# Sums of w_down's quarters formed during the first MLP product, and u kept by granule

## The chip, the cores and the metric

The kernel runs on one core of a Trainium2 chip, as one program. The metric is device time in microseconds (us), median of the runs shown; less is better. The engines are TensorE (PE, with its weight loads as PEld), VectorE (DVE), ScalarE (ACT), GpSimd (POOL) and SyncE (SP, which here only issues DMAs from a queue that it works through in order).

## The reference, cut to what matters

One inference step of a two-layer streaming encoder, for a prompt of 1024 tokens and a sample of 64 (1088 together, model width 1024). Each layer has a mixer, then cross-attention into 256 memory tokens, then a squared-ReLU MLP of width 4096. The change concerns the MLP alone:

```python
def sq_relu_mlp(h, w_up, w_down):
    return jnp.square(jax.nn.relu(h @ w_up)) @ w_down
...
x = x + cross_attn(rmsnorm(x, p['norm_cross'][layer]), mem_k[layer], mem_v[layer],
                   p['w_mq'][layer], p['w_mo'][layer])
x = x + sq_relu_mlp(rmsnorm(x, p['norm_mlp'][layer]), p['w_up'][layer], p['w_down'][layer])
```

Everything is float32. w_up is 1024x4096, w_down 4096x1024.

## The kernel before

**Precision and weights.** A float32 operand is split into a high part (an fp32r copy by ACT) and a low part (a DVE subtraction); a product is three matmuls. All weights come through one object `W` in the order of a list `plan`: `load` issues a 512 KB DMA on SP into a staging tile `st` (pool `wst`, 4 buffers), `do_split` makes the high and low parts from it (L212 on ACT, L213 on DVE) in a tile `wp` (3 buffers) or, for w_down's granules 3 to 7 of a product, `wd` (5 buffers, in the down stage's own pool). `ahead` keeps about two split tiles in front of PE.

**Order.** The code is written in program order; a tile scheduler turns it into one queue of instructions per engine, each of which runs in order, with semaphore waits between them. A tile with n buffers makes its next user wait until the release of the n-th last.

**Up stage** (`mlp_up`). Sixteen passes q, each with two w_up tiles (f = 0, 1) and three units of PE work per tile: 512 tokens of sequence half 0 and twice 288 of half 1. DVE turns a PSUM bank into `t` (L967, relu and the norm's row factor rb), ACT squares `t` into `u` (L970, L972). `u` has eight slots (four quarters, U11 to U22, and four differences T1 to T4) and two buffers. At the end of a pass POOL makes the four differences (L983, 128x544 each) and SP stores slots 0 to 6 to DRAM (L985, 1904 KB).

**The norm's rows.** PE's first unit of pass 0 is followed by `rows()`: rc is made from column sums (DVE L341, then the power -1/2 on POOL at L342), PE transposes it (L352), ACT copies it into rb. DVE's L967 of half 1 needs rb.

**Down stage** (`mlp_down`). u @ w_down is done with seven products of quarter matrices (list `SEVEN`), in two halves each, 14 steps. Step (m, half) uses four granules of weights (512 KB each, quarter (k half, n half) of w_down or a sum of quarters) and four granules of u. `load_u` reads one granule with two DMAs of 272 KB, because pass q's u lies in a DRAM tensor of its own, into `ur` (3 buffers); ACT (L259) and DVE (L262) split it into one of eight `hp` tiles. The first four granules are loaded ahead of step 0, the others during the step before. L1042, L1043, L1044 are the three matmuls; DVE adds finished banks to x. In products m = 2 to 5 a weight granule is a sum or difference of two matrices. `load` then stages both, POOL combines them (L205, 128x1024), and for m = 3 and 4 SP stores the result to DRAM (L207), because a later product reads it again:

```python
(((1, 0), "add", (1, 1)), "S1", T1, ((0, 1), (1, 1)), "add"),
(("S1", "subtract", (0, 0)), "S2", T2, ((0, 1), (1, 0), (1, 1)), "add"),
```

Both store and loads stand in SP's one queue. The stage before up is cross-attention; its last part is `project_back` with w_mo (8 weight tiles), and its tiles' space is reused by the up stage's pools.

Of the kernel before, what the change touches and what calls it, by code (L numbers as in the profile page):

```python
# [7 lines left out]
F32 = mybir.dt.float32  # L8
# [5 lines left out]
D = 1024  # L14
# [15 lines left out]
NST = 4  # L30

# [3 lines left out]
U11, U21, U22, T1, T2, T3, T4, U12 = range(8)  # L35
SEVEN = [
    (((0, 0), None, None), None, U11, ((0, 0), (0, 1), (1, 0), (1, 1)), "add"),
    (((1, 1), None, None), None, T4, ((1, 0),), "subtract"),
    (((0, 0), "subtract", (1, 0)), None, T3, ((1, 0), (1, 1)), "add"),
    (((1, 0), "add", (1, 1)), "S1", T1, ((0, 1), (1, 1)), "add"),  # L40
    (("S1", "subtract", (0, 0)), "S2", T2, ((0, 1), (1, 0), (1, 1)), "add"),
    (((0, 1), "subtract", "S2"), None, U22, ((0, 1),), "add"),
    (((0, 1), None, None), None, U21, ((0, 0),), "add"),
# [4 lines left out]
def body(ctx, tc, I, O):  # L48
# [12 lines left out]
    wst = ctx.enter_context(tc.tile_pool(name="wst", bufs=NST))  # L61
# [58 lines left out]
    def plan_mlp(l):  # L120
        for n in range(NFF):
            plan.append(((("up", l), n), "n", cols(I["w_up"][l], n * 128, 128)))
        sums = {}

        def quarter(q, g):

            w = I["w_down"][l]
            return dram(w, (4 * g + q[1]) * 128 * D + q[0] * 512, [[D, 128], [256 * D, 2], [1, 512]])

        for m, ((a, op, b), keep, *_) in enumerate(SEVEN):  # L130
            for g in range(8):
                def src(q):
                    return sums[q, g] if isinstance(q, str) else quarter(q, g)

                kept = None
                if keep:
                    kept = sums[keep, g] = scr.tile([128, 2, 512], F32, name=f"{keep}{l}_{g}")
                plan.append((("down", l, m, g), "s", (src(a), op, src(b) if op else None, kept)))

# [16 lines left out]
    class Weights:  # L156
# [5 lines left out]
        def load(self):  # L162
# [1347 lines left out]
```

## Time and profile before

| | us |
|---|---|
| median of 3 runs | 2848.53 |
| lowest, highest | 2841.72, 2851.61 |
| the profiled execution | 2846.64 |
| its span, first to last instruction | 2844.9 |
| PE busy, share of the span | 2725.1, 96% |
| DVE, ACT, POOL busy | 50%, 39%, 19% |
| mean granted TensorE clock | 0.979 |

The profiled execution is 1.9 us under the median, its span 1.7 us under its own time. Time is in the row of a group as busy us and mean ns of one instruction, then the idle time of the engine ahead of it with what ended it. A window's row gives the busy us of each engine and, behind them, the granted clock as a share of full speed. Idle time is of interest where PE waits.

### The profile page before, as it was taken

The page shows a single profiled execution, that of the slowest core. Times are in us where ns is not written, and L with a number is a line of the kernel's source. Part 1 is how long each engine was busy: PE and PEld are TensorE (multiplying, and loading weights), DVE is VectorE, ACT ScalarE, POOL GpSimd, SP SyncE. Part 2 cuts the span into 40 slices and gives each one's busy share as a digit, 9 for nine tenths or more (in the row PEclk, how much of TensorE's full clock was granted, in tenths as well). Part 3 has the DMA queues.
Part 4 walks back from the last instruction along what each step waited for, and adds up shares of the span by engine and source line. Part 5 has one row for each costly group of instructions (what it writes and reads, how often), then busy time and mean ns, then how long its engine had stood idle before and what let it go on. Part 6 is the DMA issues. An engine that isn't in the chain of part 4 may idle for free. (4 is left out here: it accounts for less than half of the span.)

```text
span 2844.9 us, 44625 instructions
## 1 busy us (share of the span) xinstructions
PE 2725.1 (96%) x18280; PEld 2545.7 (89%) x18280; DVE 1413.5 (50%) x2328; ACT 1096.5 (39%) x1929; POOL 538.4 (19%) x422
## 2 busy tenths in 40 slices
PE   8999999999999979979999999999999999799798
PEld 8978998999999979979988899889989999799798
DVE  5596756563222225445557467566522222364454
ACT  6584545343222223323337347344422222332234
POOL 3200000001222220333003013000022222123320
PEclk9999999999999989989999999999999999899899
DMA  8722232322333346777621321323223333667871
GB/s 283 221 74 82 67 105 78 105 63 87 128 128 128 130 145 222 249 262 270 185 68 28 91 64 46 93 89 93 60 100 127 128 127 127 213 223 253 281 259 71
DMA packets 355921, 395.13 MB, mean 139 GB/s; under 512 B 47632, under 2 KB 268832, under 8 KB 351620
## 3 DMA queue, kind: packets, MB, share of 16 engines
q1 hardware_dynamic: 346820, 365.23, 39.1%
q0 software_dynamic: 8896, 27.06, 2.9%
q8 instruction: 143, 2.34, 0.3%
q14 instruction: 62, 0.51, 0.1%
HBM read 299.74 MB, written 92.61 MB: 138 GB/s over the span
## 5 line engine op out<-in xcount | busy, mean ns | idle before, releaser
L242 PE MATMUL mm<-hpH,wp 128*128 128x288 f32 (+2 forms) x5952 | 1420.4, 328 | 3.9 <-DVE U L569 2.3
L242 PEld LDWEIGHTS mm<-hpH,wp 128*128 128x128 f32 x5952 | 1013.4, 188 | 83.2 <-DVE U L569 2.7
L242 PE MATMUL mm<-hpL,wp 128*128 128x288 f32 (+2 forms) x2976 | 926.2, 327 | 3.2 <-DVE hpL L317 3.2
L242 PEld LDWEIGHTS mm<-hpL,wp 128*128 128x128 f32 x2976 | 561.1, 189 | 42.4 <-DVE hpL L317 4.0
L212 ACT ACTIVATE wp<-st 128x1024 fp32r<-128x1024 f32 x282 | 297.6, 1058 | 615.4 <-PE mm L242 456.3
L213 DVE TENSOR_TENSOR wp<-st,wp 128x1024 fp32r<-128x1024 f32 x282 | 347.6, 1234 | 195.9 <-ACT wp L212 195.6
L967 DVE SCALAR_TENSOR_TENSOR t<-mm,rb 128x288 f32<-128x288 f32 (+1 forms) x184 | 99.2, 539 | 515.3 <-PE mm L242 515.3
L983 POOL TENSOR_TENSOR u<-u 128x544 f32<-128x544 f32 x128 | 218.2, 1715 | 537.2 <-ACT u L972 534.7
L205 POOL TENSOR_TENSOR st<-st 128x1024 f32<-128x1024 f32 x64 | 164.2, 2566 | 430.4 <-DMA st<-in_w_down_dram 262.0
L262 DVE TENSOR_TENSOR uhl<-ur,uhl 128x1088 fp32r<-128x1088 f32 x112 | 155.0, 1387 | 167.7 <-ACT uhl L259 167.5
L259 ACT ACTIVATE uhl<-ur 128x1088 fp32r<-128x1088 f32 x112 | 123.6, 1106 | 225.3 <-DMA ur<-u 223.2
L1042 PE MATMUL s<-uhl,wd 128*128 128x256 f32 x560 | 160.8, 288 | 31.0 <-ACT uhl L259 31.0
L1043 PE MATMUL s<-uhl,wd 128*128 128x256 f32 x560 | 161.7, 289 | 8.0 <-DVE uhl L262 8.0
L1044 PE MATMUL s<-uhl,wd 128*128 128x256 f32 x560 | 159.9, 286 | 0.0
L970 ACT ACTIVATE u<-t 128x512 f32<-128x512 f32 x64 | 40.4, 632 | 301.4 <-DVE t L967 301.4
L242 PE MATMUL s<-hpH,wp 128*128 128x288 f32 (+1 forms) x576 | 141.4, 330 | 0.0
L1042 PEld LDWEIGHTS s<-uhl,wd 128*128 128x128 f32 x560 | 109.2, 195 | 32.7 <-ACT uhl L259 32.7
L212 ACT ACTIVATE wd<-st 128x1024 fp32r<-128x1024 f32 x70 | 72.8, 1051 | 156.9 <-POOL st L205 62.5
L1042 PE MATMUL s<-uhl,wp 128*128 128x256 f32 x336 | 96.5, 291 | 36.8 <-ACT uhl L259 36.8
L213 DVE TENSOR_TENSOR wd<-st,wd 128x1024 fp32r<-128x1024 f32 x70 | 92.1, 1325 | 59.0 <-ACT wd L212 33.2
L1043 PEld LDWEIGHTS s<-uhl,wd 128*128 128x128 f32 x560 | 109.5, 196 | 9.7 <-DVE uhl L262 9.7
L342 POOL TENSOR_TENSOR rc<-rc,mhalf 128x4 f32<-128x4 f32 (+1 forms) x21 | 23.4, 1122 | 490.6 <-DVE rc L341 490.6
(364 smaller groups left out, 4725.8 us busy)
## 6 DMA issues: line engine op xcount, KB each, us to landing
st<-in_w_down_dram SPq DMA_DIRECT2D x144, 512.0 KB, 4.5
u<-u SPq DMA_DIRECT2D x32, 1904.0 KB, 5.9
ur<-u SPq DMA_DIRECT2D x224, 272.0 KB, 4.9
st<-in_w_up_dram SPq DMA_DIRECT2D x64, 512.0 KB, 4.1
st<-in_w_mq_dram SPq DMA_DIRECT2D x32, 512.0 KB, 3.6
st<-in_w_mo_dram SPq DMA_DIRECT2D x32, 512.0 KB, 3.6
S<-st SPq DMA_DIRECT2D x32, 512.0 KB, 5.9
st<-S SPq DMA_DIRECT2D x32, 512.0 KB, 4.3
```

The costliest lines, as they stand in the source:

```text
L205: pool.tensor_tensor(st, st, sts[1], getattr(OP, op))
L212: act.activation(wt[:, 0], st, AF.Copy)
L213: dve.tensor_tensor(wt[:, 1], st, f32(wt[:, 0]), OP.subtract)
L242: pe.matmul(ps, a, b, start=i == 0, stop=i == len(terms) - 1)
L259: act.activation(h, src, AF.Copy)
L262: dve.tensor_tensor(l, src, f32(h), OP.subtract)
L967: dve.scalar_tensor_tensor(t[:, :bn], ps[:, :bn], 0.0, nm.rb[:, b0:b0 + bn], OP.max, OP.mult)
L970: act.activation(slots[:, :, :256], t.rearrange("p (a b) -> p a b", a=2), AF.Square)
L983: pool.tensor_tensor(u[:, to], u[:, a], u[:, b], OP.subtract)
L1042: pe.matmul(ps, wl, uh, start=first, stop=False)
L1043: pe.matmul(ps, wh, ul, start=False, stop=False)
L1044: pe.matmul(ps, wh, uh, start=False, stop=half == 1 and g == 3 and k == 1)
```

## The change

The seven products stay, and PE's work is the same. `weights_sums(q)`, called in each up pass, loads 256 rows of w_down (two DMAs of 512 KB) into one tile `quarters` (1 buffer), POOL makes four 128x512 sums and differences in place (L947 to L950: S1, S3, S2, S4), and SP stores the tile (1 MB) to a DRAM tensor `sums`. In the down stage every weight granule is then one staged tile: 56 loads in a layer instead of 88 (72 from w_down, 16 of stored sums), with no POOL instruction (before, 32 in a layer) and no store of a sum (before, 16). u lies in DRAM by granule, so `load_u` is one DMA of 544 KB; the stores of u and of the sums go through a list `todo`, which `store()` empties at a later place in the code. The four first granules of u are loaded and split within the last up pass, after its second unit, which is why `ur` now lives in a pool around both stages. `wst` has 3 buffers instead of 4, in all stages.

```diff
+S2, S3, S4, S1 = range(4)
 SEVEN = [
-    (((0, 0), None, None), None, U11, ((0, 0), (0, 1), (1, 0), (1, 1)), "add"),
-    (((1, 1), None, None), None, T4, ((1, 0),), "subtract"),
-    (((0, 0), "subtract", (1, 0)), None, T3, ((1, 0), (1, 1)), "add"),
-    (((1, 0), "add", (1, 1)), "S1", T1, ((0, 1), (1, 1)), "add"),
-    (("S1", "subtract", (0, 0)), "S2", T2, ((0, 1), (1, 0), (1, 1)), "add"),
-    (((0, 1), "subtract", "S2"), None, U22, ((0, 1),), "add"),
-    (((0, 1), None, None), None, U21, ((0, 0),), "add"),
+    ((0, 0), U11, ((0, 0), (0, 1), (1, 0), (1, 1)), "add"),
+    ((1, 1), T4, ((1, 0),), "subtract"),
+    (S3, T3, ((1, 0), (1, 1)), "add"),
+    (S1, T1, ((0, 1), (1, 1)), "add"),
+    (S2, T2, ((0, 1), (1, 0), (1, 1)), "add"),
+    (S4, U22, ((0, 1),), "add"),
+    ((0, 1), U21, ((0, 0),), "add"),
...
-    wst = ctx.enter_context(tc.tile_pool(name="wst", bufs=NST))
+    wst = ctx.enter_context(tc.tile_pool(name="wst", bufs=3))
...
-        for m, ((a, op, b), keep, *_) in enumerate(SEVEN):
+        w = I["w_down"][l]
...
             for g in range(8):
-                def src(q):
-                    return sums[q, g] if isinstance(q, str) else quarter(q, g)
-
-                kept = None
-                if keep:
-                    kept = sums[keep, g] = scr.tile([128, 2, 512], F32, name=f"{keep}{l}_{g}")
-                plan.append((("down", l, m, g), "s", (src(a), op, src(b) if op else None, kept)))
-
+                if isinstance(q, int):
+                    src = sums[l][g][:, q]
+                else:
+                    src = dram(w, (4 * g + q[1]) * 128 * D + q[0] * 512, [[D, 128], [256 * D, 2], [1, 512]])
+                plan.append((("down", l, m, g), "s", [(slice(0, 128), None, src)]))
+    sums = [[scr.tile([128, 4, 2, 512], F32, name=f"sums{l}_{g}") for g in range(8)] for l in range(2)]
...
-            if kind == "s":
-                a, op, b, kept = pieces
-                srcs = [a] if b is None else [a, b]
-                if self.staged + len(srcs) > NST:
-                    return False
-                sts = []
-                for src in srcs:
-                    st = wst.tile([128, 1024], F32, tag="st", name="st")
-                    nc.sync.dma_start(st.rearrange("p (k n) -> p k n", n=512), src)
-                    sts.append(st)
-                self.stage[self.loaded] = sts
-                self.staged += len(srcs)
-                self.loaded += 1
-                return True
...
-            sts = self.stage.pop(self.split)
+            st = self.stage.pop(self.split)
             key, kind, pieces = plan[self.split]
-            st = sts[0]
-            if len(sts) > 1:
-                a, op, b, kept = pieces
-                pool.tensor_tensor(st, st, sts[1], getattr(OP, op))
-                if kept is not None:
-                    nc.sync.dma_start(kept, st.rearrange("p (k n) -> p k n", n=512))
...
-            self.staged -= len(sts)
+            self.staged -= 1
...
-    def mlp_up(l, norms, p):
+    def load_u(us, p, m, g):
+        ur = p.tile([128, 2, TH], F32, tag="ur", name="ur", bufs=3)
+        nc.sync.dma_start(ur, us[g][:, SEVEN[m][1]])
+        t = hpp.tile([128, 4, NT2], F32R, tag="hp", name="uhl").rearrange("p a b -> p (a b)")
+        h, lo = (t[:, 2 * TH * i:2 * TH * i + 2 * TH] for i in range(2))
+        split(h, lo, ur.rearrange("p a b -> p (a b)"))
+        return t[:, :4 * TH].rearrange("p (i k t) -> p i k t", i=2, k=2)
+
+    def mlp_up(l, norms, p, outer):
         blocks = [(0, 0, 512), (1, 0, 288), (1, 288, 288)]
-        us = []
+        us = [scr.tile([128, 7, 2, TH], F32, name=f"u{l}_{g}") for g in range(8)]
+        todo, first = [], []
+
+        def weights_sums(q):
+
+            a = p.tile([128, 4, 512], F32, tag="quarters", name="quarters", bufs=1)
+            for i in range(2):
+                nc.sync.dma_start(a[:, 2 * i:2 * i + 2],
+                                  I["w_down"][l][256 * q + 128 * i:256 * q + 128 * i + 128]
+                                  .rearrange("p (h n) -> p h n", h=2))
+
+            pool.tensor_tensor(a[:, 3], a[:, 1], a[:, 3], OP.add)
+            pool.tensor_tensor(a[:, 1], a[:, 0], a[:, 1], OP.subtract)
+            pool.tensor_tensor(a[:, 0], a[:, 3], a[:, 0], OP.subtract)
+            pool.tensor_tensor(a[:, 2], a[:, 2], a[:, 0], OP.subtract)
+            todo.append((sums[l][q // 2][:, :, q % 2], a))
+
+        def store():
+            while todo:
+                nc.sync.dma_start(*todo.pop(0))
...
                 wts[f] = W.get((("up", l), 2 * q + f))
                 for o in order[f]:
                     unit(*o)
+                    if q == 15 and o == (1, 0):
+                        store()
+                        first = [load_u(us, outer, 0, g) for g in range(4)]
                 W.ahead()
+                if f == 0:
+                    store()
             for to, a, b in ((T1, U12, U11), (T3, U22, U12), (T2, U22, T1), (T4, T2, U21)):
                 pool.tensor_tensor(u[:, to], u[:, a], u[:, b], OP.subtract)
-            d = scr.tile([128, 7, TH], F32, name=f"u{l}_{q}")
-            nc.sync.dma_start(d, u[:, :7])
-            us.append(d)
-        return us
-
-    def mlp_down(l, us, last, p):
+            todo.append((us[q // 2][:, :, q % 2], u[:, :7]))
+            weights_sums(q)
+        store()
+        return us, first
+
+    def mlp_down(l, us, first, last, p, outer):
...
-        ready = {}
-
-        def load_u(m, g):
-            ur = p.tile([128, 2, TH], F32, tag="ur", name="ur", bufs=3)
-            for i in range(2):
-                nc.sync.dma_start(ur[:, i], us[2 * g + i][:, SEVEN[m][2]])
-            t = hpp.tile([128, 4, NT2], F32R, tag="hp", name="uhl").rearrange("p a b -> p (a b)")
-            h, lo = (t[:, 2 * TH * i:2 * TH * i + 2 * TH] for i in range(2))
-            split(h, lo, ur.rearrange("p a b -> p (a b)"))
-            ready[m, g] = t[:, :4 * TH].rearrange("p (i k t) -> p i k t", i=2, k=2)
+        ready = {(0, g): t for g, t in enumerate(first)}
...
-        for g in range(4):
-            load_u(0, g)
         for i, (m, half) in enumerate(steps):
...
                     if after is not None and s == 0:
                         W.ahead(c + 1)
-                        load_u(after[0], 4 * after[1] + c)
+                        g = 4 * after[1] + c
+                        ready[after[0], g] = load_u(us, outer, after[0], g)
...
-            with phase(f"up{l}") as p:
-                us = mlp_up(l, [nexts[1], prepared(1, G_MLP + l)], p)
-            with phase(f"down{l}") as p:
+            with phase(f"mlp{l}") as outer:
+                with phase(f"up{l}") as p:
+                    up = mlp_up(l, [nexts[1], prepared(1, G_MLP + l)], p, outer)
...
-                mlp_down(l, us, last, p)
+                with phase(f"down{l}") as p:
+                    mlp_down(l, *up, last, p, outer)
```

The change also reorders queues. At the end of layer 0's cross-attention and the start of up, POOL's queue before is (o32 belongs to the last attention head, rc to the norm of half 1, u to the passes):

```order
L926 TENSOR_TENSOR o32_6191<-o32_6191 128x2x64
L342 TENSOR_TENSOR rc_6765<-rc_6765,mhalf_123 128x4
L342 TENSOR_TENSOR rc_6765<-rc_6765,mhalf_123 64x1
L983 TENSOR_TENSOR u_6780<-u_6780 128x544 x4
L983 TENSOR_TENSOR u_6965<-u_6965 128x544 x4
L983 TENSOR_TENSOR u_7150<-u_7150 128x544 x4
```

and now:

```order
L900 TENSOR_TENSOR o32_6175<-o32_6175 128x2x64
L947 TENSOR_TENSOR quarters_6958<-quarters_6958 128x512
L948 TENSOR_TENSOR quarters_6958<-quarters_6958 128x512
L949 TENSOR_TENSOR quarters_6958<-quarters_6958 128x512
L950 TENSOR_TENSOR quarters_6958<-quarters_6958 128x512
...
L950 TENSOR_TENSOR quarters_7534<-quarters_7534 128x512
L316 TENSOR_TENSOR rc_6752<-rc_6752,mhalf_107 128x4
L316 TENSOR_TENSOR rc_6752<-rc_6752,mhalf_107 64x1
L947 TENSOR_TENSOR quarters_7726<-quarters_7726 128x512
```

Between the two fences' o32 and rc there now stand the sums of passes 0 to 3, four instructions each. The u rows of the passes, one after another before, now alternate with the sums; for pass 6, tile `u_7925`:

```order
L990 TENSOR_TENSOR u_7925<-u_7925 128x544
L947 TENSOR_TENSOR quarters_9646<-quarters_9646 128x512
L948 TENSOR_TENSOR quarters_9646<-quarters_9646 128x512
L949 TENSOR_TENSOR quarters_9646<-quarters_9646 128x512
L950 TENSOR_TENSOR quarters_9646<-quarters_9646 128x512
L990 TENSOR_TENSOR u_7925<-u_7925 128x544 x3
L990 TENSOR_TENSOR u_8117<-u_8117 128x544
L947 TENSOR_TENSOR quarters_9858<-quarters_9858 128x512
```

One of pass 6's differences stands ahead of the fifteenth set of sums and three behind it.

SP's queue at the same place, the last w_mo tiles and the first w_up tiles, before:

```order
L194 DMA st_6311<-in_w_mo_dram 128x8x128
L194 DMA st_6368<-in_w_mo_dram 128x8x128
L194 DMA st_6425<-in_w_mo_dram 128x8x128
L194 DMA st_6482<-in_w_up_dram 128x8x128
L194 DMA st_6539<-in_w_up_dram 128x8x128
```

and now:

```order
L174 DMA st_6295<-in_w_mo_dram 128x8x128
L943 DMA quarters_6958<-in_w_down_dram 128x1024 x2
L174 DMA st_6352<-in_w_mo_dram 128x8x128
L955 DMA sums0_0_84<-quarters_6958 512x1x512
L174 DMA st_6409<-in_w_mo_dram 128x8x128
L943 DMA quarters_7150<-in_w_down_dram 128x1024 x2
L174 DMA st_6466<-in_w_up_dram 128x8x128
L955 DMA sums0_0_84<-quarters_7150 512x1x512
L174 DMA st_6523<-in_w_up_dram 128x8x128
L943 DMA quarters_7342<-in_w_down_dram 128x1024 x2
L174 DMA st_6580<-in_w_up_dram 128x8x128
```

Loads of `quarters` and stores of `sums` stand between the weight loads, each load of `quarters` behind the store of the one before.

SP's queue at the change from up to down, before (the u stores of passes 14 and 15, then the loads of the first granules `ur`):

```order
L985 DMA u0_14_9555<-u_9372 128x3808
L175 DMA st_9734<-in_w_down_dram 128x2x512
L175 DMA st_9773<-in_w_down_dram 128x2x512
L985 DMA u0_15_9740<-u_9557 128x3808
L999 DMA ur_9746<-u0_0_6963 128x544
L999 DMA ur_9746<-u0_1_7148 128x544
L999 DMA ur_9752<-u0_2_7333 128x544
L999 DMA ur_9752<-u0_3_7518 128x544
```

and now (the stores of passes 14 and 15 write `u0_7`, and `ur_9732` is granule 3):

```order
L955 DMA u0_7_6774<-u_9461 896x1x544
L928 DMA ur_9732<-u0_3_6770 128x1088
L928 DMA ur_9911<-u0_4_6771 128x1088
L928 DMA ur_9946<-u0_5_6772 128x1088
L928 DMA ur_9981<-u0_6_6773 128x1088
L174 DMA st_9852<-in_w_down_dram 128x2x512
L955 DMA u0_7_6774<-u_9653 896x1x544
L174 DMA st_9874<-in_w_down_dram 128x2x512
L928 DMA ur_10016<-u0_7_6774 128x1088
```

Granules 0 to 2 are loaded further up in the queue, and granules 3 to 6 stand ahead of the store of pass 15.

## Rows read from the trace of the kernel before

**Rows 1.** The page: engines, then groups by line (busy us, mean ns, idle, releaser).

```profile
PE 2725.1 (96%) x18280; PEld 2545.7 (89%) x18280; DVE 1413.5 (50%) x2328; ACT 1096.5 (39%) x1929; POOL 538.4 (19%) x422
...
L262 DVE TENSOR_TENSOR uhl<-ur,uhl 128x1088 fp32r<-128x1088 f32 x112 | 155.0, 1387 | 167.7 <-ACT uhl L259 167.5
L259 ACT ACTIVATE uhl<-ur 128x1088 fp32r<-128x1088 f32 x112 | 123.6, 1106 | 225.3 <-DMA ur<-u 223.2
```

**Rows 2.** Waits on PE: what waited, releaser; total us, count, longest.

```profile
PE s L1042 <- ACT uhl L259: 67.8, 10, 18.4
...
PE s L1043 <- DVE uhl L262: 8.0, 8, 1.4
```

**Rows 3.** Timeline, starts of the down stages: start, us, engine, line [idle <-releaser].

```profile
1056.07 0.34 SPq L985 DMA_DIRECT2D u<-u  x1
...
1068.15 1.22 PE L1042 MATMUL s<-uhl,wp 128*128 128x256 f32 x4 [18.39 <-ACT uhl L259]
...
2457.87 1.22 PE L1042 MATMUL s<-uhl,wp 128*128 128x256 f32 x4 [18.42 <-ACT uhl L259]
```

**Rows 4.** Windows, layer 0 down: us; PE, PEld, DVE, ACT, POOL; clock, DMA, GB/s.

```profile
1060.00:1080.00 20.00, 11.85 (x81) 11.65 (x82) 11.96 (x10) 10.48 (x11) 0.00 (x0) 0.68 0.92 311
1080.00:1100.00 20.00, 20.00 (x161) 20.00 (x160) 10.48 (x10) 9.84 (x10) 0.00 (x0) 1.00 0.62 209
...
1220.00:1240.00 20.00, 20.00 (x159) 19.90 (x157) 5.52 (x5) 4.13 (x4) 4.82 (x3) 1.00 0.83 299
1240.00:1260.00 20.00, 4.83 (x19) 3.94 (x19) 5.34 (x4) 4.22 (x4) 7.18 (x4) 0.58 0.68 221
1260.00:1280.00 20.00, 20.00 (x148) 20.00 (x148) 11.66 (x13) 6.30 (x6) 6.99 (x3) 0.90 0.88 297
1280.00:1300.00 20.00, 17.92 (x133) 17.52 (x132) 9.37 (x15) 5.56 (x6) 6.15 (x3) 0.91 0.82 275
```

**Rows 5.** Timeline, end of layer 0 cross-attention and start of up.

```profile
623.83 0.35 DVE L262 TENSOR_TENSOR hpL<-o,hpH 128x64 fp32r<-128x64 f32 x2
...
675.88 2.50 POOL L342 TENSOR_TENSOR rc<-rc,mhalf 128x4 f32<-128x4 f32 x2 [52.61 <-DVE rc L341]
677.92 0.65 PE L352 MATMUL t<-ident,rc 128*128 128x128 f32 x4 [1.18 <-POOL rc L342]
```

**Rows 6.** DMA issues by tile: count, KB each, median us to landing.

```profile
u<-u SPq DMA_DIRECT2D x32, 1904.0 KB, 5.9
...
st<-in_w_mv_dram SPq DMA_DIRECT2D x16, 512.0 KB, 5.1
```

**Rows 7.** Source view of L175, loads of one w_down quarter (512 KB).

```profile
DMA to landing us min/median/max: 3.4/4.5/8.6
```

**Rows 8.** Source view of L207, stores of a sum (512 KB).

```profile
DMA to landing us min/median/max: 2.9/5.9/7.4
```

**Rows 9.** Source view of L983, subtractions of u: ns min/median/max.

```profile
L983 POOL TENSOR_TENSOR u<-u x128: 1323/1705/2082, 690.7 to 2444.4; 128x544 f32<-128x544 f32 x128
```

**Rows 10.** Timeline, first passes of layer 0's up stage, ACT, DVE and POOL.

```profile
674.92 0.63 ACT L970 ACTIVATE u<-t 128x512 f32<-128x512 f32 x1 [1.75 <-DVE t L967]
...
690.33 1.22 DVE L213 TENSOR_TENSOR wp<-st,wp 128x1024 fp32r<-128x1024 f32 x1 [0.56 <-ACT wp L212]
690.71 2.07 POOL L983 TENSOR_TENSOR u<-u 128x544 f32<-128x544 f32 x1 [12.32 <-ACT u L972]
...
707.47 1.06 ACT L212 ACTIVATE wp<-st 128x1024 fp32r<-128x1024 f32 x1 [2.24 <-PE mm L242]
...
731.03 1.06 ACT L212 ACTIVATE wp<-st 128x1024 fp32r<-128x1024 f32 x1 [2.19 <-PE mm L242]
```

**Rows 11.** Windows, a stretch of the up stage, columns as in Rows 4.

```profile
740.00:760.00 20.00, 20.00 (x119) 18.11 (x118) 4.68 (x7) 4.31 (x7) 6.82 (x4) 1.00 0.40 145
```

**Rows 12.** Timeline of the memory stage, splits of successive weight tiles.

```profile
95.08 1.23 DVE L213 TENSOR_TENSOR wp<-st,wp 128x1024 fp32r<-128x1024 f32 x1 [0.67 <-ACT wp L212]
...
103.50 1.05 ACT L212 ACTIVATE wp<-st 128x1024 fp32r<-128x1024 f32 x1
```

More of the change, by code (lines that the diff above doesn't have):

```diff
@@ L122, in plan_mlp @@
             plan.append(((("up", l), n), "n", cols(I["w_up"][l], n * 128, 128)))
[L123 to L128, printed above, removed]
-        for m, ((a, op, b), keep, *_) in enumerate(SEVEN):
-            for g in range(8):
-                def src(q):
-                    return sums[q, g] if isinstance(q, str) else quarter(q, g)
-                kept = None
-                if keep:
-                    kept = sums[keep, g] = scr.tile([128, 2, 512], F32, name=f"{keep}{l}_{g}")
-                plan.append((("down", l, m, g), "s", (src(a), op, src(b) if op else None, kept)))
+        w = I["w_down"][l]
+        for m, (q, *_) in enumerate(SEVEN):
+            for g in range(8):
+                if isinstance(q, int):
[4 more added lines that the diff above has]
+    sums = [[scr.tile([128, 4, 2, 512], F32, name=f"sums{l}_{g}") for g in range(8)] for l in range(2)]
     plan_dense(I["w_in_even"][0], IN_ORDER, ("in", 0))
@@ L189, in load @@
                     dst = st.rearrange("p (k n) -> p k n", n=256)
+                elif kind == "s":
+                    dst = st.rearrange("p (k n) -> p k n", n=512)
                 elif kind == "q":
@@ L194, in load @@
                 nc.sync.dma_start(dst, src)
-            self.stage[self.loaded] = [st]
+            self.stage[self.loaded] = st
             self.loaded += 1
@@ L980, in mlp_up @@
                     unit(*o)
+                    if q == 15 and o == (1, 0):
+                        store()
+                        first = [load_u(us, outer, 0, g) for g in range(4)]
                 W.ahead()
+                if f == 0:
+                    store()
             for to, a, b in ((T1, U12, U11), (T3, U22, U12), (T2, U22, T1), (T4, T2, U21)):
                 pool.tensor_tensor(u[:, to], u[:, a], u[:, b], OP.subtract)
-            d = scr.tile([128, 7, TH], F32, name=f"u{l}_{q}")
-            nc.sync.dma_start(d, u[:, :7])
-            us.append(d)
-        return us
-    def mlp_down(l, us, last, p):
+            todo.append((us[q // 2][:, :, q % 2], u[:, :7]))
[3 more added lines that the diff above has]
+    def mlp_down(l, us, first, last, p, outer):
         W.more = p
         steps = [(m, h) for m in range(7) for h in range(2)]
-        ready = {}
-        def load_u(m, g):
-            ur = p.tile([128, 2, TH], F32, tag="ur", name="ur", bufs=3)
-            for i in range(2):
-                nc.sync.dma_start(ur[:, i], us[2 * g + i][:, SEVEN[m][2]])
-            t = hpp.tile([128, 4, NT2], F32R, tag="hp", name="uhl").rearrange("p a b -> p (a b)")
-            h, lo = (t[:, 2 * TH * i:2 * TH * i + 2 * TH] for i in range(2))
-            split(h, lo, ur.rearrange("p a b -> p (a b)"))
-            ready[m, g] = t[:, :4 * TH].rearrange("p (i k t) -> p i k t", i=2, k=2)
+        ready = {(0, g): t for g, t in enumerate(first)}
         banks = {}
         def evacuate(m, s, c):
-            to, sign = SEVEN[m][3:]
+            to, sign = SEVEN[m][2:]
             h = WIDTH[s] // 2
```

1 line of the change is left out of this document (removed).

## The prediction

> **What bounds the kernel now.** I read the engines' busy time first: PE is busy for 96% of the span, DVE for half of it, POOL for a fifth [rows 1]. Only time in which PE waits can be won, so the waits on PE came next. Two rows matter: matmuls of the down stage waited 67.8 us in ten pieces for L259, the high part of a granule of u, and 8.0 us in eight pieces for L262, its low part [rows 2]. The timeline puts the two longest at the start of each down stage, 18.39 us in layer 0 and 18.42 in layer 1 [rows 3]: 36.8 of the 75.8. The other 39.0 lie inside the two stages. The windows show where. After the first window, eight in a row from 1080 to 1240 us keep PE full (the first and the last of them stand in [rows 4]); from 1240 to 1260 PE is busy 4.83 of 20 us, and it is short again at 1280. This is where products m = 3 and 4 come, whose weights need two quarters, a POOL instruction and a store. Steps 0 to 3, whose weights are one plain quarter, lie in the full windows.
>
> A wait costs more than its length. The granted clock is 1.00 in the full windows (2.4 GHz) and 0.68, 0.58, 0.90 and 0.91 in those with a wait, so part of each ran at 1.2 GHz [rows 4]. I count in matmuls: a full window has 161, one per 0.124 us.
>
> The sum is made against the profiled execution, 2846.6 us with a span of 2844.9, which is 1.9 us under the median 2848.5; all savings are taken off the median.
>
> **A. The start of the down stage.** Before, granule 0 could not be read until u of pass 15 was stored at 1056.07, since the loads stand behind that store; PE started at 1068.15 [rows 3]. Window 1060 to 1080 has 81 matmuls, 80 short: 9.9 us, of which 8.15 are idle, so the slower clock took 1.8 [rows 4]. Two layers lose 36.8 + 3.6 = 40.4 us. Now three granules are read in mid-up and the fourth ahead of pass 15's store. What is late next are the weights: the third weight tile is split only behind three splits of u (1.11 us each on ACT, 1.39 on DVE [rows 1]), some 4.2 us on DVE, and two weight splits of 1.2 [rows 10], 6.6 in all. PE has 48 matmuls from the first two granules meanwhile, 6.0 us; hand-overs come on top, so I leave a wait of 2.5 per layer (0 to 6). Gain 40.4 - 5.0 = **35.4**. The granules of step 1 have the 24 us of step 0 (192 matmuls) to arrive, and cost nothing.
>
> **B. Inside the down stage.** The three disturbed windows have 19 + 148 + 133 = 300 matmuls instead of 483, 183 short or 22.7 us, for 15.17 + 2.08 = 17.25 us of idle time [rows 4]: a factor of 1.31. The 39.0 us of waits thus cost about **51**. After the change each granule of products 2 to 5 is one load and two splits, exactly what steps 0 to 3 have now, and these show no wait. SP, too, loses 32 second loads and 16 stores per layer. The cover is one load (4.5 us median [rows 7]) behind PE's 6 us per weight tile; I claim all of it.
>
> **C. The new work at the norm.** POOL's queue now has four sets of sums ahead of rc, the norm's power, and PE's transposes wait for rc. Before, POOL did nothing for 52.61 us ahead of it, and PE followed 2.0 us behind it, already 1.18 late [rows 5]. So the four sets have a hole, and the question is whether they fit. The first load of quarters waits for the space of cross-attention's last tiles, free at 623.83 + 0.35 = 624.2; PE started at 677.92 [rows 5]. That is 53.7 us. One set needs:
> - the loads: one issue of 0.34 [rows 3], then 4.5 [rows 7]: 4.8 (bounds 3.7 and 8.9, by that row's ends);
> - four POOL instructions. A subtraction of 128x544 takes 1.32 to 2.08 us, 1.705 in the middle [rows 9]; scaled to 512 columns 1.6, so 6.4 (bounds 5.0 and 8.3);
> - the store, since quarters has one buffer and the next load waits for it: 512 KB took 2.9 us at best [rows 8] and 1904 KB took 5.9 [rows 6], so by a straight line 1 MB takes 4.0, with the issue 4.3 (bounds 3.2 and 6.2).
>
> The cycle is 4.8 + 6.4 + 4.3 = 15.5 to 15.6. Four loads, four sets, three stores and rc to PE make 19.4 + 25.6 + 13.0 + 2.0 = 60.0 us, 6.3 more than there is; with 1 us of slow clock (by the factors of A and B 0.6 to 2), **7.2 per layer, 14.4 in all**. Between its bounds the chain is 46 to 89 us, so this term alone can be 0 or 36 per layer; I take the middle rows, since nothing in this stretch (DMA queue and POOL otherwise idle) speaks for either end.
>
> **D. The sums in mid-up.** POOL is busy 6.82 of 20 us in this stretch [rows 11], and its own time is no bound: a set leaves 9.1 us of each cycle in which POOL would wait for DMAs, and four subtractions of u (6.8) fit in there. But queues are in order: three of pass 6's four subtractions stand behind the fifteenth set. That ends at 624.2 + 14 x 15.6 + 11.2 = 853.8; stores of u that stand directly ahead of a load of quarters may hold the chain by 12 more; then three subtractions (5.1) and the store's landing (5.9 [rows 6]): 876.8. Who waits is ACT, which refills that u tile in pass 8. A pass takes 731.03 - 707.47 = 23.56 us, and the first Square was at 674.92 [rows 10], so it is due at 863.4; PE can run half a pass (11.8) ahead on its banks, and is itself 7.2 late by C: 882.4. Margin 5.6 us, **cost nothing**. For a cycle longer by x us a layer pays 7.2 + 3x + (11x - 5.6 where positive).
>
> **E. Staging.** With three `st` buffers a weight load waits for the split three tiles back, not four. The tightest stage is the memory stage: a split ends at 95.08 + 1.23 = 96.3, and the split three tiles on starts at 103.50 [rows 12]; 7.2 us for a load of 5.1 [rows 6]. Covered there with 2 to spare; a few late loads may cost 0 to 3. I take **1**.
>
> Sum: 35.4 + 51 - 14.4 - 1 = 71.0. 2848.5 - 71.0 = **2777.5 us**.
>
> **Rivals.**
> 1. *The sums fit in front of the norm.* With sets of 5.0 to 5.5 us and loads near 4 the chain is under 53.7 and C is nothing: 2848.5 - 35.4 - 51 + 1 = 2763. For it: the shortest rows. Against it: every term has to be short.
> 2. *The sums' cycle becomes the pace of the up stage*, by D's formula. At 17.5 us (POOL at its slowest row, 8.3, alone gives that) a layer pays 7.2 + 5.7 + 15.3 = 28.2, and the time is 2848.5 - 85.4 + 56.4 = 2819.5. It decides against the change where a layer pays 42.7, at x = 2.9, a cycle of 18.5; at 20 us the time is 2848.5 - 85.4 + 126.4 = 2889.5, slower than before. For it: only about 6 us of margin, one buffer, and three engines in turn. Against it: 18.5 needs two of three terms near their upper bound.
>
> A mechanism for it would be POOL held by DVE. At 690.71 a subtraction that began inside a DVE split (690.33 to 691.55) took 2.07 us [rows 10], against 1.32 at best [rows 9]. If every POOL instruction waited for one such DVE instruction of 1.22, a set would take 4 x (1.32 + 1.22) = 10.2, the cycle 19.4, and the time 2873. DVE is busy only 4.68 of 20 us there [rows 11], so I hold few of them to wait and give this 0.05, within rival 2. The Trainium skill ("SBUF — State Buffer", section "SBUF: two separate sides") states that DVE, with two inputs in SBUF, and GpSimd share a port pair as an exclusive lock, held for a whole instruction; by that rule the 2.07 is a wait, and the trace agrees as far as one row can.
>
> 3. *The waits inside the down stage stay.* If they come from the loads of u and not from sums, with DMA 0.68 to 0.88 busy there [rows 4], only A is won: 2848.5 - 35.4 + 14.4 + 1 = 2828.5; with half of B, 2803. Against it: the first four steps load as much u and don't wait.
>
> **How the numbers follow.** Forecast 0.46, rival 1 0.12, rival 2 0.30 (of it 0.07 slower than before and 0.03 at no change), rival 3 0.12. A measurement of this kernel can tell about 0.3%, 8.5 us, from no change; 2840 to 2857 is "same". Faster 0.46 + 0.12 + 0.20 + 0.12 = 0.90, same 0.03, slower 0.07. The range goes from 2757, rival 1 with A's wait gone, to 2828, which leaves out the longer half of rival 2 and little else.
>
> **What would show it.** A: the waits of 18.4 us at the first matmul of each down stage are gone, at most 6 stays. B: windows of the down stage are full, POOL's 128x1024 group is gone, waits for L259 and L262 sum to under 10. C: PE's rb transposes wait for POOL's rc for about 7 us, twice; the first four sets begin near 624 and follow one another by 15.6. D: windows of the up stage stay at 20.00, and no ACT Square waits for a u store. The prediction is wrong if sets follow one another by more than 16 us and PE waits in up past pass 0, or if PE still waits at m = 3 and 4.

## The result, and the profile after

The changed kernel takes 2807.2 us (median, 2806.3 to 2810.2) beside 2847.1 for the kernel before, a ratio of 0.986, interval 0.984 to 0.988: faster by 40 us, where 71 were forecast (2777.5). The time lies inside the range of 2757 to 2828, and the sign was right. All of the hoped-for gain arrived; a bill of 46 us, three times the forecast one, came with it, in the up stage.

The page of the profiled execution (2806.5 us), the line of the engines and the DMA issues, and the waits on PE (total us, count, longest):

```profile
PE 2720.7 (97%) x18280; PEld 2540.8 (91%) x18280; DVE 1414.6 (50%) x2328; ACT 1094.2 (39%) x1929; POOL 535.8 (19%) x486
...
u<-u SPq DMA_DIRECT2D x32, 1904.0 KB, 8.4
...
quarters<-in_w_down_dram SPq DMA_DIRECT2D x64, 512.0 KB, 5.2
sums<-quarters SPq DMA_DIRECT2D x32, 1024.0 KB, 5.4
st<-in_w_up_dram SPq DMA_DIRECT2D x64, 512.0 KB, 6.6
```

```profile
PE t L326 <- POOL rc L316: 21.8, 6, 9.9
PE mm L216 <- DVE t L969: 13.1, 5, 4.5
...
PE t L310 <- DVE ss L300: 4.7, 2, 2.7
PE s L1038 <- DVE wp L187: 4.4, 2, 2.2
```

and the norm's row before:

```profile
PE t L352 <- POOL rc L342: 7.0, 6, 3.2
```

The waits for L259 and L262, 75.8 us [rows 2], are gone from the list. In their place PE waits for the norm's rc (21.8, against 7.0 before, six pieces each), in the up stage for DVE to empty a PSUM bank (13.1, new), and just ahead of rc for DVE's column sums ss (4.7, new; the last section comes back to it). The last row is the wait for the third weight tile at the start of down, 2.2 us in each layer.

To see where each stretch's time went I set the two timelines side by side, by the matmul with the same number in PE's queue (each trace holds 18280). The marks lie where PE runs at full speed in both, so that a step holds a wait together with the slow clock behind it:

| matmul in | before, us | after, us | shift | step |
|---|---|---|---|---|
| layer 0, cross-attention | 620.04 | 620.53 | +0.50 | +0.5 |
| up, pass 2, behind the norm | 740.10 | 753.75 | +13.65 | +13.2 |
| up, pass 13 | 1000.12 | 1025.67 | +25.55 | +11.9 |
| down, step 1 | 1100.10 | 1108.88 | +8.78 | -16.8 |
| down, near the end | 1420.02 | 1400.58 | -19.44 | -28.2 |
| layer 1, cross-attention | 2000.01 | 1982.49 | -17.52 | +1.9 |
| up, behind the norm | 2090.10 | 2085.16 | -4.94 | +12.6 |
| up, pass 15 | 2430.00 | 2433.22 | +3.21 | +8.2 |
| down, step 1 | 2500.07 | 2484.68 | -15.39 | -18.6 |
| down, near the end | 2820.00 | 2778.52 | -41.48 | -26.1 |
| end of the span | 2844.9 | 2804.7 | -40.2 | +1.3 |

In each layer the steps of up are the losses at the norm (25.7 us in both layers) and in mid-up (20.1), and the steps of down the gains at its start (35.4) and inside it (54.3).

**At the norm.** Timeline of POOL (start, us, line), the first four sets and rc, with SP's rows of the first cycles and PE's transposes:

```profile
629.77 1.28 POOL L947 TENSOR_TENSOR quarters<-quarters 128x512 f32<-128x512 f32 x1 [6.01 <-DMA quarters<-in_w_down_dram]
...
634.73 1.68 POOL L950 TENSOR_TENSOR quarters<-quarters 128x512 f32<-128x512 f32 x1
648.09 1.30 POOL L947 TENSOR_TENSOR quarters<-quarters 128x512 f32<-128x512 f32 x1 [11.67 <-DMA quarters<-in_w_down_dram]
...
666.45 1.29 POOL L947 TENSOR_TENSOR quarters<-quarters 128x512 f32<-128x512 f32 x1 [11.49 <-DMA quarters<-in_w_down_dram]
...
683.69 1.26 POOL L947 TENSOR_TENSOR quarters<-quarters 128x512 f32<-128x512 f32 x1 [11.01 <-DMA quarters<-in_w_down_dram]
...
688.92 1.53 POOL L316 TENSOR_TENSOR rc<-rc,mhalf 128x4 f32<-128x4 f32 x2
```

```profile
624.80 0.82 SPq L943 DMA_DIRECT2D quarters<-in_w_down_dram  x2
...
636.45 0.62 SPq L955 DMA_DIRECT2D sums<-quarters  x1
637.16 0.57 SPq L174 DMA_DIRECT2D st<-in_w_mo_dram  x1
642.00 0.82 SPq L943 DMA_DIRECT2D quarters<-in_w_down_dram  x2
642.92 0.38 SPq L174 DMA_DIRECT2D st<-in_w_up_dram  x1
```

```profile
689.99 1.11 PE L326 MATMUL t<-ident,rc 128*128 128x128 f32 x4 [9.93 <-POOL rc L316]
```

The first load starts at 624.80, 0.6 us from the forecast. The sets then follow one another by 18.3, 18.4 and 17.2 us, not 15.6. The first set's chain can be read off: load 624.80 to 629.77 (5.0), four instructions to 636.41 (6.6), and the next load at 642.00, when the store has landed (5.6). Over four sets the loads take 5.5, the sets 6.2 and the stores 5.8 us in the mean, where 4.8, 6.4 and 4.3 were taken. SP's rows show a 512 KB weight load issued directly behind each store and each load of quarters, so no transfer here is alone; how much of their time that costs isn't shown by these rows.

**In mid-up.** Windows of layer 0 (us; PE, PEld, DVE, ACT, POOL busy; clock, DMA share, GB/s), and ACT's longest wait for a tile of u:

```profile
680.00:700.00 20.00, 10.07 (x51) 8.63 (x51) 1.25 (x3) 1.34 (x3) 7.47 (x7) 0.66 0.60 207
...
840.00:860.00 20.00, 18.12 (x94) 16.04 (x93) 4.80 (x6) 4.71 (x8) 10.44 (x7) 0.91 0.57 201
860.00:880.00 20.00, 18.36 (x122) 17.07 (x121) 3.90 (x6) 3.32 (x6) 6.47 (x5) 1.00 0.95 328
880.00:900.00 20.00, 17.41 (x98) 15.16 (x96) 2.83 (x4) 1.39 (x2) 11.01 (x8) 1.00 0.59 196
900.00:920.00 20.00, 18.07 (x108) 17.10 (x109) 6.07 (x8) 4.71 (x8) 15.86 (x11) 0.91 0.70 226
920.00:940.00 20.00, 20.00 (x119) 18.11 (x118) 5.21 (x7) 4.72 (x9) 6.79 (x4) 1.00 0.71 217
...
1240.00:1260.00 20.00, 20.00 (x165) 20.00 (x164) 12.18 (x16) 8.14 (x8) 0.00 (x0) 1.00 0.56 192
1260.00:1280.00 20.00, 20.00 (x162) 20.00 (x161) 12.33 (x16) 8.14 (x8) 0.00 (x0) 1.00 0.40 135
```

```profile
900.75 0.63 ACT L972 ACTIVATE u<-t 128x512 f32<-128x512 f32 x1 [19.13 <-DMA u<-u]
```

In windows 840 to 920 PE is idle for 8.0 us in all, where the windows on either side (720 to 840 and 920 to 1040) are full; with the slow clock in two of the four, the table has 11.9 us for it. ACT waited 19.13 us for a store of u to land before it could overwrite the tile; that is the chain of term D (store behind differences, differences behind a set), and the sets' starts from the first (629.77) to the fifteenth (881.86) give a cycle of 252.1 / 14 = 18.0 us. After the sixteenth set, at 920, the windows are full again. And windows 1240 to 1280, two of the worst of before [rows 4], are full at clock 1.00.

### The profile page after: what moved, and what is told of

It is laid out like the page before. It is cut to its first block, busy times and chain, and to the rows that moved or that the text cites. A ratio compares the mean times of both kernels' runs of the same rounds, so it can differ in the third digit from the quotient of the medians.

```text
span 2804.7 us, 44507 instructions
## 1 busy us (share of the span) xinstructions
PE 2720.7 (97%) x18280; PEld 2540.8 (91%) x18280; DVE 1414.6 (50%) x2328; ACT 1094.2 (39%) x1929; POOL 535.8 (19%) x486
## 5 line engine op out<-in xcount | busy, mean ns | idle before, releaser
L216 PE MATMUL mm<-hpH,wp 128*128 128x288 f32 (+2 forms) x5952 | 1428.3, 329 | 16.9 <-DVE t L969 13.1
L187 DVE TENSOR_TENSOR wp<-st,wp 128x1024 fp32r<-128x1024 f32 x282 | 357.0, 1267 | 277.2 <-ACT wp L186 274.8
L990 POOL TENSOR_TENSOR u<-u 128x544 f32<-128x544 f32 x128 | 203.8, 1606 | 233.3 <-ACT u L974 230.8
L1039 PE MATMUL s<-uhl,wd 128*128 128x256 f32 x560 | 156.5, 280 | 0.0
L1038 PE MATMUL s<-uhl,wd 128*128 128x256 f32 x560 | 156.1, 279 | 0.0
L1040 PE MATMUL s<-uhl,wd 128*128 128x256 f32 x560 | 156.0, 279 | 0.0
L236 DVE TENSOR_TENSOR uhl<-ur,uhl 128x1088 fp32r<-128x1088 f32 x112 | 146.2, 1307 | 16.5 <-ACT uhl L233 16.4
L216 PEld LDWEIGHTS s<-hpH,wp 128*128 128x128 f32 x576 | 98.1, 188 | 8.0 <-ACT hpH L233 0.3
L1038 PEld LDWEIGHTS s<-uhl,wd 128*128 128x128 f32 x560 | 105.3, 188 | 0.0
L1039 PEld LDWEIGHTS s<-uhl,wd 128*128 128x128 f32 x560 | 105.1, 188 | 0.0
L1040 PEld LDWEIGHTS s<-uhl,wd 128*128 128x128 f32 x560 | 105.0, 187 | 0.0
```

The source lines that it names most:

```text
L187: dve.tensor_tensor(wt[:, 1], st, f32(wt[:, 0]), OP.subtract)
L216: pe.matmul(ps, a, b, start=i == 0, stop=i == len(terms) - 1)
L236: dve.tensor_tensor(l, src, f32(h), OP.subtract)
L990: pool.tensor_tensor(u[:, to], u[:, a], u[:, b], OP.subtract)
L1038: pe.matmul(ps, wl, uh, start=first, stop=False)
L1039: pe.matmul(ps, wh, ul, start=False, stop=False)
```

## Experiments

Theory 1: both losses come from POOL's queue, which is worked through in order. rc stands behind four sets of a chain that takes 17 to 18 us a set, and later the differences of u stand behind sets. Theory 2: the added traffic (1 MB in and 1 MB out per pass) delays w_up's tiles and u's stores wherever POOL's work stands. All kernels were timed beside the kernel before; ratios are against it, with their 95% interval. That kernel took 2847.1 us beside the changed one, 2852.5 beside `held`, `held_from_4`, `late_u` and `early_u_alone`, and 2848.0 beside the rest, so kernels are compared by their ratios. A table behind experiment 7 has the marks of every kernel.

**1. One set for each pass (`held`).** A small POOL instruction makes each set wait for the differences of the pass before:

```diff
-        def weights_sums(q):
+        def weights_sums(q, u):
...
             a = p.tile([128, 4, 512], F32, tag="quarters", name="quarters", bufs=1)
+            if u is not None:
+                pool.tensor_tensor(a[:, :, 0:1], u[:, T1:T4 + 1, 0:1], u[:, T1:T4 + 1, 0:1], OP.add)
...
+        u = None
         for q in range(16):
+            weights_sums(q, u)
...
-            weights_sums(q)
```

> The sums of pass q now wait for the differences of pass q-1 (a small POOL addition of 128x4 writes into quarters first), so at most one set stands in front of the norm's rc and one set in each pass. All the arithmetic and all the transfers stay. Theory 1 (POOL's in-order queue: rc stands behind four sets whose cycle is 17 to 18 us, and later the differences of u stand behind sets): PE's waits for rc fall from 9.9 and 7.5 us to about 1, the waits at DVE's t in mid-up vanish, and the time falls by the 24 us of the norm and the 24 us of mid-up to about 2760 (2750 to 2772). Theory 2 (the added DMA traffic is what delays up's weights and stores, wherever POOL's work stands): only the part at the norm goes, about 2783, and the waits in mid-up stay.

Measured: 2774.0 us, ratio 0.973 (0.971 to 0.974). All transfers are still made, and the waits for rc (1.2 in each layer, as before the change) and in mid-up are gone: theory 2 falls as it was put. (The sets are also spread over 16 passes here, so the transfers come less densely; experiment 4 has them denser.) By the ratio the time is 2769 beside the changed kernel's 2807, within theory 1's range and 9 us over its figure, since a wait grew, for the third weight tile of the down stage (4.4 in the changed kernel):

```profile
PE s L1041 <- DVE wp L187: 12.8, 2, 6.5
```

The rows of POOL and SP show why: the store of the last set waits for POOL, and the loads of u (granules 3 to 5), whose splits stand ahead of that tile's, come behind it.

```profile
1046.89 1.31 POOL L952 TENSOR_TENSOR quarters<-quarters 128x512 f32<-128x512 f32 x1
...
1048.22 0.52 SPq L957 DMA_DIRECT2D sums<-quarters  x1
...
1048.84 2.77 SPq L928 DMA_DIRECT2D ur<-u  x3
```

**2. Four sets early, the rest held (`held_from_4`).** In the loop above:

```diff
-            weights_sums(q, u)
+            for j in range(4) if q == 0 else [q + 3] if q < 13 else []:
+                weights_sums(j, u)
```

> Sets 0 to 3 run as early as in the changed kernel, ahead of rc; from set 4 on each waits for the differences of a pass (set 4 for pass 0, and so on). Theory 1: the rc waits stay (8 to 10 us in each layer) and only the mid-up waits vanish: about 2783 (2775 to 2792). Theory 2 (DMA traffic): mid-up waits stay, about 2807.

Measured: 2784.9 us, ratio 0.976 (0.975 to 0.978). PE waits 8.0 us for rc in each layer and not at all in mid-up. The two losses are separate, and removing the one in mid-up is worth 0.986 - 0.976 = 1.0%, 28 us with some 7 either way; by the marks the MLPs are 22.4 shorter, 20.1 of it in mid-up.

**3. Two sets early, one for each pass, none in the last (`held_two_ahead`).**

```diff
-            weights_sums(q, u)
+            for j in range(2) if q == 0 else [q + 1] if q < 15 else []:
+                weights_sums(j, u)
```

> As the held kernel, but sets 0 and 1 both run ahead of the norm and set q+1 waits for the differences of pass q-1, so the last set belongs to pass 14 and no longer stands, with its store, in front of the loads of granules 3 to 6 and of the last weights in SP's queue. If that queue position is what made the first weights of the down stage late (6.5 and 6.3 us instead of 2.2 in the held kernel), the wait falls back to 2.2 and the time falls by 2 x 4.2 and some slow clock, about 9 us, to 0.969 to 0.970 of the kernel before (about 2761). The rival, that two sets ahead of rc are already too many, would show a wait for rc of more than 1.2 us and no gain.

Measured: 2762.8 us, ratio 0.970 (0.968 to 0.971), the fastest of all, 85 us under the kernel before. Its waits on PE in layer 0, from 600 to 1100 us:

```profile
PE s L1042 <- DVE wp L187: 2.2, 1, 2.2
PE t L326 <- POOL rc L316: 1.2, 1, 1.2
...
```

Only the 2.2 of term A and the 1.2 of the kernel before are left: two sets fit in front of the norm, four don't. Against experiment 2 this prices the wait at the norm: 0.9763 - 0.9695 = 0.7%, 19 us for both layers, slow clock with it, with some 6 either way; the marks have 21.9 for it in experiment 2 and nothing here. Against experiment 1 it prices the place of the last set: 0.9727 - 0.9695 = 0.3%, 9 us, as expected.

**4. Two buffers for quarters (`two_quarters`).** `bufs=2` for quarters, `bufs=2` for ur.

> The changed kernel with two buffers for quarters instead of one; to make room, ur has two buffers instead of three. The scheduler now puts six sets ahead of rc. Theory 1 (the cycle of 17 to 18 us is load, set and store one after another on one buffer): a pair of sets takes about 19 us instead of 34, six sets end near 680, rc waits 1 to 4 us a layer, the waits in mid-up vanish: 2807 - 48 + 2 x 3 = 2765, ratio 0.968 to 0.976. Rival (SP's queue, in which a store waits for POOL and all later loads behind it, keeps the cycle where it is): six sets then take over 90 us, rc waits over 30 us a layer and the time is over 2840.

Measured: 2782.8 us, ratio 0.977 (0.975 to 0.978), 0.1% above the expected ratios. The mid-up waits are gone, as theory 1 says, but PE waits longer for rc than expected, 11.7 us in each layer. POOL's rows, first instructions of sets 0, 2 and 4 and rc:

```profile
630.84 1.29 POOL L947 TENSOR_TENSOR quarters<-quarters 128x512 f32<-128x512 f32 x1 [6.25 <-DMA quarters<-in_w_down_dram]
...
654.18 1.28 POOL L947 TENSOR_TENSOR quarters<-quarters 128x512 f32<-128x512 f32 x1 [10.04 <-DMA quarters<-in_w_down_dram]
...
678.08 1.35 POOL L947 TENSOR_TENSOR quarters<-quarters 128x512 f32<-128x512 f32 x1 [10.89 <-DMA quarters<-in_w_down_dram]
...
688.65 1.53 POOL L316 TENSOR_TENSOR rc<-rc,mhalf 128x4 f32<-128x4 f32 x2
```

A pair takes 23.3 to 23.9 us, 11.8 a set: less than 18, so the single buffer was part of the cycle, but more than the 9.5 expected. Between pairs POOL waits 10.04 us for a load, and the loads of quarters now land in 7.1 us in the median (5.2 in the changed kernel), the loads being issued among stores. Since six sets stand ahead of rc, the norm waits no less. The rival falls: six sets took 57.8 us from 630.84 on, not over 90. And so does what was left of theory 2: a window of this kernel's mid-up shows more DMA traffic than three of the changed kernel's four short ones, with PE full, and PE has no wait at all between 700 and 1050 us.

```profile
820.00:840.00 20.00, 20.00 (x130) 18.73 (x129) 4.44 (x7) 4.22 (x7) 11.37 (x8) 1.00 0.93 303
```

**5. The early u undone, twice.** `late_u` takes the three lines with `first` out of the last up pass and loads the granules at the start of `mlp_down`:

```diff
-                    if q == 15 and o == (1, 0):
-                        store()
-                        first = [load_u(us, outer, 0, g) for g in range(4)]
...
-        ready = {(0, g): t for g, t in enumerate(first)}
+        ready = {(0, g): load_u(us, outer, 0, g) for g in range(4)}
```

> The changed kernel without its early loads: the first four granules of u are loaded and split at the start of the down stage again. Theory 1: the 18.4 us wait comes back in each layer with 1.8 us of slow clock, and the 2.2 us wait for the third weight tile goes: 2807 + 2 x 18.0 = 2843 (2836 to 2849). Rival: with one DMA of 544 KB for a granule and no sums to store, the start of the down stage is quick anyway, and the early loads are worth under 10 us a layer: below 2828.

Measured: 2809.5 us, ratio 0.985 (0.984 to 0.987), the same as the changed kernel. The time is where the rival had it, but not for its reason: the wait of 18 us did not come back, because the scheduler put the loads of granules 0 to 2 into the up stage all the same (at 764, 818 and 875 us). Its only wait at the start of down is the changed kernel's, for a weight tile:

```profile
PE s L1035 <- DVE wp L187: 4.4, 2, 2.2
```

`u_in_down_pool` is late_u with `ur` in the down stage's own pool (`p` for `outer` in both calls):

> The late_u kernel again, with ur back in the down stage's own pool. In late_u the scheduler still moved the loads of granules 0 to 2 into the up stage, since ur's space was free there; here they stand behind the last store of u in SP's queue and wait for the up stage's space. If that is what the early start rests on, PE waits about 18 us for L233's high part at the start of each down stage again and the time is 2807 + 2 x 16 to 2 x 18 = 2841 (ratio 0.995 to 1.002). If the one DMA per granule was what mattered, the wait is under 10 and the ratio stays below 0.992.

Measured: 2836.7 us, ratio 0.996 (0.994 to 0.997), 26 us over the changed kernel. The wait is back:

```profile
1079.63 0.53 SPq L955 DMA_DIRECT2D u<-u  x1
1080.21 3.05 SPq L928 DMA_DIRECT2D ur<-u  x3
```

```profile
1091.33 1.22 PE L1035 MATMUL s<-uhl,wp 128*128 128x256 f32 x4 [18.00 <-ACT uhl L233]
```

The loads follow the last store of u, as in the kernel before [rows 3]. So the early start rests on the space that `ur` has in a pool around both stages, not on where the code calls `load_u`. The price by the ratios, 26 with some 7 either way, is below the 32 to 36 expected. By the marks the start of down lost 35.7 us in the two layers, all that A had won, and mid-up gave 4.0 back (PE's waits there are 4.1 us in layer 0 against 8.0).

**6. The early u alone (`early_u_alone`).** The kernel before with `load_u` (its two DMAs kept) called in the last up pass, and ur in a pool around both stages:

```diff
+                    if q == 15 and o == (1, 0):
+                        first = [load_u(us, outer, 0, g) for g in range(4)]
...
-        for g in range(4):
-            load_u(0, g)
```

> The kernel before with one thing changed: the first four granules of u (still two DMAs of 272 KB each) are loaded and split within the last up pass. The sums stay in the down stage. Theory 1 (the two halves of the change are independent): 2847 - 35.4 = 2812 (2806 to 2820), with the waits inside the down stage (39 us in the two layers) as before. Rival: the waits at products 3 and 4 come partly from a start that is late, or the early start only moves them forward: they grow or shrink by more than 10 us.

Measured: 2814.8 us, ratio 0.987 (0.985 to 0.988): 37.6 us by the ratio, where 35.4 were taken for term A. Its waits on PE:

```profile
PE s L1042 <- ACT uhl L259: 33.1, 8, 11.8
PE s L1043 <- DVE uhl L262: 8.0, 8, 1.4
...
PE s L1042 <- DVE wp L213: 4.4, 2, 2.2
```

33.1 + 8.0 = 41.1 us are left of the waits inside the down stage, 39.0 before; the early start neither cures nor feeds them. What cures them is in the rest of the change. SP's own waits in the kernel before, from 1195 to 1300 us, point at the sums:

```profile
SPq L175 <- DMA st<-in_w_down_dram: 32.2, 11, 5.3
SPq L175 <- POOL st L205: 28.9, 11, 3.4
```

SP waits there at loads of weights, for POOL's sums and for loads into staging tiles, and the loads of u (L999) stand behind them in its queue without a wait of their own. No run has the single load of a granule without the sums' move, so that its share is nothing is argued: products without sums load u by the same two DMAs in full windows [rows 4].

**7. Four staging buffers (`wst4`).** `bufs=4` for `wst`.

> The changed kernel with four staging buffers for weights again. If the third buffer's loss costs what was taken (1 us), nothing is to be seen: ratio 0.984 to 0.988, as the changed kernel's. If weight loads that wait in SP's queue behind sums are part of the mid-up waits, a fourth buffer lets them be issued earlier and wins 5 us or more.

Measured: 2802.7 us, ratio 0.984 (0.9825 to 0.9855). The interval overlaps that of the changed kernel (0.984 to 0.988), and the waits for rc (10.2 and 8.5) and in mid-up (12.3) stand as they were, so a fourth buffer does not cure them. From nothing to 13 us is left open by the ratios. By the marks the MLPs are 3.1 us shorter than in the changed kernel; the stretch ahead of them can't be compared, since it shifts from kernel to kernel (-1.5 and +2.8 us with four buffers, +0.5 to +6.9 with three); a cost of some us there isn't excluded.

**All kernels by the marks.** Time lost (+) or won (-) against the kernel before, in us for both layers, from the profiled execution of each:

| kernel | norm | mid-up | start of down | inside down |
|---|---|---|---|---|
| changed kernel | +25.7 | +20.1 | -35.4 | -54.3 |
| `held` | 0.0 | 0.0 | -24.3 | -54.3 |
| `held_from_4` | +21.9 | 0.0 | -33.8 | -54.3 |
| `held_two_ahead` | -0.1 | 0.0 | -36.9 | -54.3 |
| `two_quarters` | +26.2 | 0.0 | -35.8 | -54.3 |
| `late_u` | +25.5 | +20.6 | -35.4 | -54.3 |
| `u_in_down_pool` | +25.4 | +16.1 | +0.3 | -54.3 |
| `early_u_alone` | 0.0 | 0.0 | -36.9 | +2.7 |
| `wst4` | +24.7 | +19.5 | -36.9 | -54.3 |

The last column stands still wherever the sums are formed in the up stage, and the gain is missing only in `early_u_alone`, which keeps them in the down stage. Mid-up goes to nothing while the norm's loss stays (`held_from_4`, `two_quarters`), and the start of down goes without the others (`u_in_down_pool`): the terms are separate. In `held_two_ahead` the whole gain is there and the bill is gone.

## Why the prediction was right, and where it was too good

The time lies in the range, but 30 us over the forecast, and the prediction's own sign of being wrong came up: sets followed one another by 17 to 18 us, over 16, and PE waited in up past pass 0. The account holds for A and B; it is too small for C and wrong for D. The range took the result in because it had been drawn wide enough for the milder half of rival 2.

- **A, the start of down.** Right in mechanism and size: the 18.4 us are gone, the wait for the third weight tile came at 2.2 us where 2.5 was taken, and the marks give the 35.4 us that were taken (alone 36.9, by the ratio 37.6). What the prediction did not see is that the pool, not the call's place, makes it possible (experiment 5).
- **B, inside down.** Right. The marks give 54.3 us where 51 were taken: the 39.0 us of waits cost 1.39 times their length, not 1.31.
- **C, the norm.** The mechanism was right, the size short: 25.7 us against 14.4. The chain of four loads, four sets, three stores and rc was put at 60.0 us; it took 65.2 from the first load's issue. By terms: loads 21.8 for 19.4, sets 25.0 for 25.6, stores 17.3 for 13.0, rc to PE 1.1 for 2.0. So the step that failed is the straight line for the store (4.3 taken, 5.8 measured), and beside it the load (4.8 taken, 5.5 measured). Both lie inside the bounds that the prediction gave (3.2 to 6.2 and 3.7 to 8.9). The prediction says that it takes the middle rows, but its line for the store starts from the shortest of [rows 8], 2.9; the median there, 5.9, with the issue gives its upper bound, 6.2. The store's landing takes 5.4 us in the median in all eight kernels that have it, however closely the sets follow one another. The load's median does go with the kernel (4.2 us in `held`, 5.2 in the changed kernel, 7.1 in `two_quarters`), and the "otherwise idle" DMA queue was a slip: the list of SP's queue shows two weight loads in each cycle.
- **D, mid-up.** "Margin 5.6 us, cost nothing" was wrong: 11.9 + 8.2 = 20.1 us. The chain was named as it is, but the margin was worked out at a cycle of 15.6. At 18.0 the fifteenth set is 14 x 2.4 = 34 us later, and a margin of 5.6, with PE itself 6 us later than forecast, doesn't cover that. The formula, put at x = 2.4, gives 35 us a layer for C and D; 25.1 and 20.7 were measured. It is too high by the 12 us taken for stores of u ahead of loads: the fifteenth set ended at 887.8, and 624.2 + 14 x 18.0 + 11.2 is 887.4 without them; the formula then gives 23. Two more terms were off and nearly cancel: the Square of pass 8 was due at 867.2 in the kernel before, not 863.4, since pass 0 is longer than the rest, and PE ran about 8 us ahead, not 11.8 (that Square started at 900.75, 19.9 late against 867.2 and the norm's shift of 13.65, and PE lost 11.9). This is rival 2 in its mild form, which had 0.20 of that rival's 0.30.
- **E.** 1 us taken; experiment 7 and the table leave it open.

In sum 35.4 + 54.3 - 25.7 - 20.1 - 3.7 = 40.2, the span's difference (3.7 are the three steps outside the MLP). Of the rivals, 1 fell (no wait at the norm), 3 fell (no wait inside down is left), and rival 2's cycle came to 18.0 of the 18.5 at which it was to decide against the change. That was not as near as it looks, since the formula was too high; but "needs two of three terms near their upper bound" was wrong as well, for the load's bound of 8.9 alone makes the cycle 19.7.

## What to carry to other kernels

Work moved onto an idle engine is not free if that engine's queue is in order and something short and urgent stands behind it: look up what the scheduler puts there, and bind background work to the pace of the stage (here two sets ahead and then one for each pass, worth 1.7%, 48 us) rather than let it run as early as its inputs allow. A background chain of load, compute and store on one buffer has to be priced with the middle row of every term, and the margin of whatever waits behind it has to be worked out over the whole range of its cycle: an error of 2.4 us in one set was 34 us at the fifteenth. And a transfer can start early only if its destination is free early: with this scheduler the pool in which a tile lives decided that, not the line that issues the load.

## What the runs showed of the hardware that was not expected

In the changed kernel 102 of POOL's 128 instructions of 128x512 began outside any DVE instruction on two inputs in SBUF, and took 1.26 to 1.30 us. Of the 26 that began inside one, 22 took 1.68 to 2.35: longer by what was left of the DVE instruction, less 0.13 to 0.15 us (with 0.54 left 0.39 longer, with 1.20 left 1.06). Three of the other four began in its last 0.16 us, one at the same moment as it. DVE waits likewise: eight of the nine splits of 128x1024 that began inside one of these instructions took 1.56 to 2.15 us, where the rest take 1.23 in the middle. Timelines of POOL and DVE in the changed kernel's first set:

```profile
631.13 1.29 POOL L948 TENSOR_TENSOR quarters<-quarters 128x512 f32<-128x512 f32 x1
632.50 2.16 POOL L949 TENSOR_TENSOR quarters<-quarters 128x512 f32<-128x512 f32 x1
634.73 1.68 POOL L950 TENSOR_TENSOR quarters<-quarters 128x512 f32<-128x512 f32 x1
```

```profile
631.74 1.76 DVE L187 TENSOR_TENSOR wp<-st,wp 128x1024 fp32r<-128x1024 f32 x1 [0.64 <-ACT wp L186]
633.43 1.84 DVE L300 TENSOR_TENSOR ss<-ss,sq 128x576 f32<-128x576 f32 x1
...
639.25 0.75 DVE L300 TENSOR_TENSOR ss<-ss,sq 128x576 f32<-128x576 f32 x1
```

The split that began at 631.74, while POOL's L948 ran, took 1.76 instead of 1.23; L949, which began beside that split, took 2.16; the next DVE instruction, L300, beside L949, took 1.84 instead of 0.75; and L950 beside that one 1.68. The Trainium skill ("SBUF — State Buffer", section "SBUF: two separate sides") calls the port pair that the two engines share an exclusive lock, which the other side has to wait for; this alternation agrees with it. It is not why the cycle came out longer than forecast: the four sets ahead of the norm took 6.6, 6.9, 6.2 and 5.3 us, and their mean of 6.2 is below the 6.4 taken. But it reached PE: beside the third set two of DVE's L291 took 3.70 us, where the same two took 1.55 before, and the column sums ss that stand behind them came late (PE's new wait of 2.7 us in layer 0). There it cost nothing more, since rc was later still; with two sets ahead of the norm, PE does not wait for ss.

```profile
667.33 1.55 DVE L317 SCALAR_TENSOR_TENSOR hpL<-x,gcol,hpH 128x576 fp32r<-128x576 f32 x2 [1.75 <-PE mm L242]
...
667.82 3.70 DVE L291 SCALAR_TENSOR_TENSOR hpL<-x,gcol,hpH 128x576 fp32r<-128x576 f32 x2 [1.53 <-PE mm L216]
```

The first of these two rows is the kernel before's, the second the changed kernel's.
